# Partial sums of a feed-forward's block products kept in PSUM banks, with ScalarE copying the intermediate sums

## The chip, the cores and the metric

The kernel runs on one core of a Trainium2 chip. The metric is the device time of one execution in microseconds, the median of several runs. One execution was also recorded by the hardware profiler; its span, from the first to the last instruction, is what the rows below are counted in.

## The reference

One layer of a diffusion backbone on 2048 latent tokens of width 1024, in float32, with 256 context tokens. What matters here is the channel mixer behind the second norm:

```
def swiglu(u, wg, wu, wd):
    return (jax.nn.silu(u @ wg) * (u @ wu)) @ wd

x = layer_norm(ALPHA * x + gt1 * mix, ln1_g, ln1_b)
u2 = modulate(layer_norm(x), sh2, sc2)
x = layer_norm(ALPHA * x + gt2 * swiglu(u2, w_ffn_gate, w_ffn_up, w_ffn_down), ln2_g, ln2_b)
```

`w_ffn_gate` and `w_ffn_up` are 1024 x 2816, `w_ffn_down` is 2816 x 1024. The mixer in front of it (a Fourier group and a retention group with one input and one output projection) is not touched.

## The kernel before

The kernel has four phases: A (conditioning, input projection, mixing), B (output projection and norms), C (gate and up of the feed-forward) and D (down projection and the last norm). The change is in phase C.

**Products.** A float32 product is made of float16 matmuls: each operand is split into a high and a low half, and `mm3` issues three matmuls (high by high, high by low, low by high) of 128x128 by 128x512 into one PSUM bank. Gate and up are each computed in Winograd's form of a 2 x 2 block product: seven products of blocks take the place of eight, named A11, A12, S2, S3, A22, S1, S4 after their left operands, and 0 to 6 in this order. With P1 to P7 their results, the four quadrants are C11 = P1 + P2, C12 = U + P5 + P3, C21 = U + P7 + P4, C22 = U + P7 + P5 with U = P1 + P6, where P1 = A11, P2 = A12, P6 = S2, P7 = S3, P4 = A22, P5 = S1, P3 = S4.

**Loops.** `HJ` = 11 tiles j of the hidden width (each a pair of ff tiles, j and j + 11). For each j there is a gate pass (`gu` 0) and an up pass (`gu` 1), here called units: 22 in all. In a unit each of the seven products is computed for both halves of the tokens (`sb` 0 and 1, operands `u2b` and `u2a` in the rows), half beside half, so 14 products of 4 x 3 = 12 matmuls. Two units differ: in the first (j 0, gate) and in the last (j 10, up) all seven products of half 0 come before those of half 1.

**What follows a product.** `prod` takes the next bank of a ring of eight (`ALL_BANKS`, all banks of PSUM), and `post` empties it: product 0 is copied to SBUF as `p` by ScalarE (L1286); on VectorE, product 2 makes `a` = p + P6 (L1291), product 3 makes `b` = a + P7 (L1294), product 5 adds to `a` in place (L1298), and products 1, 4, 5 and 6 complete a quadrant each in `done`: an add (L1276 in a gate unit, L1280 in an up unit) followed by ScalarE's Silu (L1277) in a gate unit, or by a VectorE multiplication with the gate's result (L1281) in an up unit. In an up unit `h_part` then makes the operands of the hidden block: sums on GpSimd (L1243 to L1245, L1251), stores from the SP queue (L1232), and for the operands S1 and S4 a split into float16 halves through the tile `ht`, of which there is one (L1131 on ScalarE, L1132 on VectorE).

**Weights beside it.** The weights of a unit are loaded in two DMAs into `raw` tiles (a ring of three, L1078), combined on GpSimd (L963 to L966) and split into halves by ScalarE and VectorE (`split`, L148 and L149) into `ws` tiles (a ring of twelve). After each tile j but the last, `down` prepares a part of the down projection's weights through the same two rings: it loads `raw` (L1143), multiplies it by the gate row on GpSimd (L1144), makes the operands on GpSimd (L1157 to L1172), splits them into `wdo` (two tiles, L148, L149) and stores these from the SP queue (L1154, L1165).

**Order.** The order of each engine's instructions is fixed when the kernel is built, by a planner that goes by the order of the program and by the times that it assumes. On the chip each engine takes its own instructions in that order, and an instruction that waits holds up all behind it on its engine.

Of the kernel before, what the change touches and what calls it, by code (L numbers as in the profile page):

```python
# [12 lines left out]
ALU = mybir.AluOpType  # L13
# [66 lines left out]
def layer_kernel(ctx: ExitStack, tc: tile.TileContext, a, out):  # L80
# [32 lines left out]
    # the banks of PSUM: by their use in phase A, and in turn after it  # L113
# [11 lines left out]
    # a ring for weights, raw and split, that every phase loads through  # L125
# [25 lines left out]
    def mm3(o, sh, sl, mh, ml, first, last):  # L151
        T.matmul(o, sh, mh, start=first, stop=False)  # L152
        T.matmul(o, sh, ml, start=False, stop=False)  # L153
        T.matmul(o, sl, mh, start=False, stop=last)  # L154
# [41 lines left out]
    # biases of shift and scale, (sublayer, k tile, shift | 1 + scale), times SU  # L196
# [5 lines left out]
    def gemv(pool, raw, v, cols, tag):  # L202
        """acc[p, n] = sum_k raw[p, k, n] * silu(c)[p, k]; the sum over p is left to TensorE."""
# [6 lines left out]
    # shift and scale columns of the first sublayer: smod[v][k] = (SU*shift, SU*(1+scale))  # L210
# [20 lines left out]
    def u_part(pool, xs, hi, lo, s, k, tag, on_act):  # L231
        """One k tile, modulated, transposed and split: hi + lo = SU * u^T."""
# [16 lines left out]
    def w_units(tiles, segs, n):  # L249
        """Units of work that load and split weights, two k tiles each, to tiles [P, (hi, lo), n]."""  # L250
# [22 lines left out]
    # startup: the modulation arrives k tile by k tile, and the first projection follows it  # L273
# [9 lines left out]
    # the modulation waits partly where the later blocks' tokens will be  # L283
# [39 lines left out]
    for k in range(KT):  # L323
# [3 lines left out]
        if k < ON_PE:  # L327
            # TensorE has little to do as yet: it makes the context's columns too
# [26 lines left out]
    # the first chunks' queries, keys and values wait where the context's tokens will be  # L355
# [22 lines left out]
    # decays: log_sigmoid, then every power that is needed  # L378
# [29 lines left out]
    def powers(dst, col, dirn):  # L408
        """dst[:, h] = exp(lg[h] * idx[:, col])"""
# [9 lines left out]
    # both directions, one on each half of the partitions  # L419
# [25 lines left out]
    def fourier(j):  # L445
# [11 lines left out]
        # bins 0, 8, 4  # L457
# [7 lines left out]
        # bins 2, 6  # L465
# [6 lines left out]
        # odd bins  # L472
# [23 lines left out]
        # DFT over the channels of a group  # L496
# [13 lines left out]
        # DFT over positions; the real part, transposed  # L510
# [23 lines left out]
    # retention group  # L534
# [7 lines left out]
    # units of work that fill in beside the projections  # L542
# [5 lines left out]
    def ctx_cols(k):  # L548
        """Shift and scale columns of the context."""
# [22 lines left out]
    def gate_row(gi, c):  # L572
# [4 lines left out]
        # the bias is a row of brow  # L577
# [14 lines left out]
    def keys(p, kh, vt):  # L592
        """Decayed keys against values, both directions stacked: [f | b] on the partitions."""
# [12 lines left out]
    LAG = 3  # steps from a block's last gate to its transposition  # L606

    class Pair:
# [6 lines left out]
        def decays(self):  # L615
            """Decays since each token's chunk was entered, along the free axis."""
# [17 lines left out]
        def context(self):  # L634
            """Keys and values of the context's chunks: the first states."""
# [20 lines left out]
        def scan1(self, d, j):  # L656
            """The state that reaches chunk j, from the chunk before it in direction d."""
# [10 lines left out]
        def scans(self, most):  # L668
            """Scan along the order of the first pass, as far as chunks and context are there."""
# [6 lines left out]
        # first pass: one chunk's projection and what follows it, in stages  # L676
# [33 lines left out]
        def turn(self, t, c):  # L710
            # the keys of both heads, and each head's queries twice, for both directions
# [31 lines left out]
        # second pass  # L743
# [9 lines left out]
        def cross(self, two, c):  # L753
# [12 lines left out]
            # the squares stand where the result will  # L766
# [78 lines left out]
        def second_pass(self, order, side):  # L845
            """A step gates one chunk, then takes up the two chunks before, and later the block that they complete."""
# [43 lines left out]
    def go(s):  # L890
        """One more stage of the units that were started, all of them at the end of a pass."""
# [58 lines left out]
    def right(qa, qb):  # L950
        """The right factor's quadrants, raw (11, 12) and (21, 22), to its seven operands, scaled and split."""
# [15 lines left out]
        for src in (t1, q1, q2, q0, q3):  # L967
            op(src)
        return ops
# [31 lines left out]
    def out_proj(t, between=None, last=False):  # L1001
# [12 lines left out]
        if last:  # L1014
            # the rest of the first tokens' operands, in the place of what the projection used
# [24 lines left out]
    def u2_part(sb, i, xh):  # L1040
        """Modulated, transposed, summed and split: the left factor's operands for a pair of token tiles."""
# [31 lines left out]
    def w_raws(src, j):  # L1073
        """Loads what the seven operands of a gate or up weight, ff tiles j and j + NJ / 2, are made of."""
# [10 lines left out]
    # the banks of the feed-forward's first products, and those that stay for the last tokens' operands  # L1085
# [17 lines left out]
    def prod(w, o, sb, tags):  # L1103
        ps = bank(tags)
        pv = ps.rearrange("p (i t) -> p i t", i=4)
        for k in range(4):
            mm3(pv, w[o][:, 0, k], w[o][:, 1, k], u2[sb][o][:, :, k, 0], u2[sb][o][:, :, k, 1], k == 0, k == 3)
        return ps

    # the feed-forward's first products fill TensorE while the last tokens are normed  # L1110
# [10 lines left out]
    # the down projection takes Winograd's form twice, one within the other, in its first five products:  # L1121
    # two levels of operands of the ff tiles 0 to 9 of a half, one level of the last; one level in ONE
# [459 lines left out]
```

## Time and profile before

| | |
|---|---|
| median of 3 runs | 2224.63 us (2222.48 to 2227.11) |
| span of the profiled execution | 2215.0 us |
| TensorE matmul busy | 93% of the span |
| VectorE busy | 71% |
| ScalarE busy | 35% |
| GpSimd busy | 38% |
| mean granted TensorE clock | 0.97 of full speed |

The profiled execution's own time was not recorded apart from its span; the median of the runs is 9.6 us above that span. Busy shares are averages over four phases with different limits. The last gate and up product of phase C ends at 1793.9 us of the span.

### The profile page before, as it was taken

What the parts mean: (1) busy time and instruction counts of PE and PEld (TensorE: products, weight loads), DVE (VectorE), ACT (ScalarE), POOL (GpSimd) and SP (SyncE); (2) the same over time, 40 slices, a digit from 0 to 9 for tenths busy, and PEclk for the clock granted to TensorE, in tenths of its full rate; (3) what the DMA queues carried; (4) which work ended last, traced back from release to release, by engine and by line L of the source; (5) the groups of instructions that cost most, each with busy time, mean ns of one, the idle gap of its engine ahead of it and who ended that gap; (6) DMA issues with size and microseconds to landing.
All of it is one profiled execution on the core that took longest, in us unless ns stands there. A gap on an engine that the chain in (4) does not pass through costs nothing.

```text
span 2215.0 us, 31357 instructions
## 1 busy us (share of the span) xinstructions
PE 2054.5 (93%) x11678; PEld 1187.5 (54%) x11678; DVE 1582.7 (71%) x2900; ACT 767.3 (35%) x1356; POOL 839.9 (38%) x838
## 2 busy tenths in 40 slices
PE   7987999999999999789999999999999889898998
PEld 5555676577558444334444444444444358786743
DVE  7667584765688677777757666676765787988856
ACT  5634542332223344442233233233223223333222
POOL 3402321221221266466446545554646342222110
PEclk8998999999999999989999999999999999999999
DMA  9402321221242556523333434334334296678543
GB/s 288 168 3 76 105 79 48 77 61 49 62 120 101 194 190 237 190 99 112 130 127 110 139 106 140 115 119 142 107 128 153 72 294 200 203 221 267 207 139 132
DMA packets 308745, 305.21 MB, mean 138 GB/s; under 512 B 14752, under 2 KB 248048, under 8 KB 307440
## 3 DMA queue, kind: packets, MB, share of 16 engines
q1 hardware_dynamic: 301776, 287.08, 40.4%
q10 hardware_dynamic: 6816, 16.12, 2.0%
q8 instruction: 92, 1.51, 0.3%
q14 instruction: 61, 0.50, 0.1%
HBM read 200.25 MB, written 102.90 MB: 137 GB/s over the span
## 4 chain that ended last, share of the span: by engine, by line
DVE 32%; PE 31%; DMA 14%; POOL 11%; issue 6%; ACT 4%; SPq 2%; POOLq 0%; DVEq 0%; ACTq 0%
PE proj L152 6%; PE proj L154 6%; PE proj L153 6%; DVE ws L149 4%; DVE sg L1281 3%; DVE wdo L149 3%; DMA raw<-in_w_ffn_down_dram 3%; DVE macc L207 3%; DVE ho L1132 2%; DMA wd<-wdo 2%; DMA h<-h 2%; POOL raw L1144 2%; DMA raw<-in_w_ffn_gate_dram 2%; DVE c L1280 2%; POOL us L1062 1%
## 5 line engine op out<-in xcount | busy, mean ns | idle before, releaser
L152 PE MATMUL proj<-ws,uhi 128*128 128x512 f16 (+1 forms) x768 | 250.7, 326 | 1.1 <-ACT vt L700 0.4
L153 PE MATMUL proj<-ws,uhi 128*128 128x512 f16 (+1 forms) x768 | 250.4, 326 | 0.0
L154 PE MATMUL proj<-ws,ulo 128*128 128x512 f16 (+1 forms) x768 | 250.3, 326 | 0.0
L153 PEld LDWEIGHTS <-ws 128*128 128x128 f16 x1296 | 128.3, 99 | 207.6 <-issue 54.3
L152 PEld LDWEIGHTS <-ws 128*128 128x128 f16 x1296 | 128.3, 99 | 160.1 <-issue 10.7
L154 PEld LDWEIGHTS <-ws 128*128 128x128 f16 x1296 | 128.1, 99 | 156.2 <-issue 7.7
L149 DVE SCALAR_TENSOR_TENSOR ws<-raw,ws 128x512 f16<-128x512 f32 x186 | 152.4, 831 | 56.8 <-ACT ws L148 56.7
L149 DVE SCALAR_TENSOR_TENSOR wdo<-raw,wdo 128x256 f16<-128x256 f32 (+1 forms) x100 | 68.4, 714 | 119.7 <-ACT wdo L148 119.7
L148 ACT ACTIVATE ws<-raw 128x512 f16<-128x512 f32 x186 | 110.9, 623 | 104.8 <-DMA raw<-in_w_ffn_gate_dram 31.1
L152 PE MATMUL misc<-u2b,ws 128*128 128x512 f16 x296 | 115.2, 389 | 30.3 <-DVE b L1294 22.1
L1131 ACT CAST ho<-h 128x1280 f16<-128x1280 f32 x60 | 75.2, 1257 | 120.6 <-DMA h<-h 36.9
L152 PE MATMUL proj<-u2a,ws 128*128 128x512 f16 x296 | 112.2, 379 | 3.7 <-DVE c L1280 3.1
L154 PE MATMUL misc<-u2b,ws 128*128 128x512 f16 x296 | 115.5, 390 | 0.0
L153 PE MATMUL misc<-u2b,ws 128*128 128x512 f16 x296 | 115.4, 390 | 0.0
L167 POOL TENSOR_TENSOR rstd<-ve,mhalf 128x1 f32<-128x1 f32 x66 | 38.3, 588 | 200.6 <-DVE ve L165 177.7
L1144 POOL TENSOR_TENSOR raw<-raw,gt 128x512 f32<-128x512 f32 x40 | 56.2, 1415 | 149.9 <-DMA raw<-in_w_ffn_down_dram 135.6
L153 PE MATMUL proj<-u2a,ws 128*128 128x512 f16 x296 | 112.2, 379 | 0.0
L154 PE MATMUL proj<-u2a,ws 128*128 128x512 f16 x296 | 112.2, 379 | 0.0
L207 DVE SCALAR_TENSOR_TENSOR macc<-raw,sil,macc 128x128 f32<-128x128 f32 x308 | 109.1, 387 | 3.2
L1132 DVE TENSOR_TENSOR ho<-h,ho 128x1280 f16<-128x1280 f32 x60 | 103.0, 1719 | 9.2 <-ACT ho L1131 8.9
L152 PEld LDWEIGHTS <-uhi 128*128 128x128 f16 x768 | 75.8, 99 | 44.0 <-issue 2.4
L153 PEld LDWEIGHTS <-uhi 128*128 128x128 f16 x768 | 75.4, 98 | 43.4 <-issue 2.2
(529 smaller groups left out, 5664.7 us busy)
## 6 DMA issues: line engine op xcount, KB each, us to landing
h<-h SPq DMA_DIRECT2D x40, 640.0 KB, 4.4
raw<-in_w_mod_dram SPq DMA_DIRECT2D x44, 512.0 KB, 4.1
wd<-wdo SPq DMA_DIRECT2D x50, 448.0 KB, 2.5
wd<-wd SPq DMA_DIRECT2D x33, 640.0 KB, 8.7
h<-sg SPq DMA_DIRECT2D x66, 256.0 KB, 2.0
raw<-in_w_ffn_gate_dram SPq DMA_DIRECT2D x22, 512.0 KB, 4.6
raw<-in_w_ffn_up_dram SPq DMA_DIRECT2D x22, 512.0 KB, 4.6
h<-hs SPq DMA_DIRECT2D x44, 256.0 KB, 2.1
```

What stands on the lines that cost most here:

```text
L148: S.activation(hi, raw, AF.Copy, scale=scale)
L149: V.scalar_tensor_tensor(lo, raw, scale, hi, ALU.mult, ALU.subtract)
L152: T.matmul(o, sh, mh, start=first, stop=False)
L153: T.matmul(o, sh, ml, start=False, stop=False)
L154: T.matmul(o, sl, mh, start=False, stop=last)
L167: pows.append(G.tensor_tensor(rstd, ve, mhalf[:, 0:n], ALU.pow).ins)
L207: V.scalar_tensor_tensor(acc, raw[:, k], sil[:, v, k : k + 1], acc, ALU.mult, ALU.add)
L1131: S.copy(dst[:, 0], src)
L1132: V.tensor_tensor(dst[:, 1], src, dst[:, 0], ALU.subtract)
L1144: G.tensor_tensor(raw[:, k], raw[:, k], gv, ALU.mult)
L1280: V.tensor_tensor(c, src, ps, ALU.add)
L1281: V.scalar_tensor_tensor(dst, c, HS, dst, ALU.mult, ALU.mult)
```

## The change

Seven of the eight banks' uses get a fixed place, and sums are formed by TensorE in the bank. For each half of the tokens a bank x collects P1, then P6, P7 and P4 on top, and a bank z collects P5, then P3 on top; P2 has a bank of its own. Between two products that go onto x, ScalarE copies the sum that stands there: `p` = P1, `a` = P1 + P6, `b` = P1 + P6 + P7. The adds that made `a` and `b` and the in-place add to `a` on VectorE go away, and quadrant C21 is complete in x, so that its add goes away too: Silu or the multiplication reads the bank directly. x is `proj` for half 0 and `misc` for half 1 (two banks each), z is `s0` or `s1`, and A12 uses `tq` or `zt`. The order of the products becomes A11, A12, S2, S1, S3, A22, S4, and `right` makes the weights' operands in that order. The sums on GpSimd in `h_part` are made when C21 is complete instead of C22, since C21 now comes last of the two.

The first unit keeps the old way for half 0 (`alone`). For half 1 of the first unit and both halves of the last, where one half's products follow each other, A22 goes to a bank of its own (`loose`) and C21 keeps its add. All comments were dropped as well.

```
-    def mm3(o, sh, sl, mh, ml, first, last):
-        T.matmul(o, sh, mh, start=first, stop=False)
+    def mm3(o, sh, sl, mh, ml, first, last, onto=False):
+        T.matmul(o, sh, mh, start=first, stop=False, skip_group_check=onto)
...
+    ORDER = (A11, A12, S2, S1, S3, A22, S4)
...
-        for src in (t1, q1, q2, q0, q3):
+        for src in (t1, q0, q1, q2, q3):
             op(src)
-        return ops
+        return [ops[ORDER.index(o)] for o in range(7)]
...
-    def prod(w, o, sb, tags):
-        ps = bank(tags)
+    def prod(w, o, sb, tags, onto=None):
+        ps = bank(tags) if onto is None else onto
...
-            mm3(..., k == 0, k == 3)
+            mm3(..., onto is None and k == 0, k == 3, onto is not None)
...
             elif quad == 3:
+                h_out(sb, A22, h[3])
+            elif quad == 2:
                 sums[sb] = mk(cq, [P, 3, 512], tag="hs", bufs=2)
                 s1, s2, s3 = (sums[sb][:, o] for o in range(3))
-                h_out(sb, A22, h[3])
...
+            def done(sb, quad, src, ps):
+                dst = sg[sb][:, quad]
+                if gu == 0:
+                    if src is None:
+                        S.activation(dst, ps, AF.Silu, scale=ISU)
+                    else:
                         V.tensor_tensor(dst, src, ps, ALU.add)
                         S.activation(dst, dst, AF.Silu, scale=ISU)
+                    return
+                if src is None:
+                    V.scalar_tensor_tensor(dst, ps, HS, dst, ALU.mult, ALU.mult)
+                else:
+                    c = mk(cq, [P, 512], tag="c", bufs=2)
+                    V.tensor_tensor(c, src, ps, ALU.add)
+                    V.scalar_tensor_tensor(dst, c, HS, dst, ALU.mult, ALU.mult)
+                h_part(sb, quad)
+
+            def keep(sb, name, ps):
+                t = st[sb][name] = mk(cq, [P, 512], tag=name, bufs=2)
+                S.copy(t, ps)
...
+            def product(o, sb, loose=False):
+                d = st[sb]
+                if o == A11:
+                    d["x"] = prod(w, o, sb, (("proj", "misc")[sb],))
+                    keep(sb, "p", d["x"])
+                elif o == A12:
+                    done(sb, 0, d["p"], prod(w, o, sb, (("tq", "zt")[sb],)))
+                elif o == S2:
+                    keep(sb, "a", prod(w, o, sb, None, d["x"]))
+                elif o == S1:
+                    d["z"] = prod(w, o, sb, (("s0", "s1")[sb],))
+                elif o == S3:
+                    keep(sb, "b", prod(w, o, sb, None, d["x"]))
+                    done(sb, 3, d["b"], d["z"])
+                elif o == A22 and loose:
+                    done(sb, 2, d["b"], prod(w, o, sb, (("tq", "zt")[sb],)))
+                elif o == A22:
+                    done(sb, 2, None, prod(w, o, sb, None, d["x"]))
+                else:
+                    done(sb, 1, d["a"], prod(w, o, sb, None, d["z"]))
...
-                for o in range(7):
+                for o in ORDER:
                     for sb in range(2):
                         product(o, sb)
```

## Rows read from the trace of the kernel before

**Rows 1.** The page: the span, and the busy time, share of the span and instructions of three engines.

```profile
span 2215.0 us, 31357 instructions
...
PE 2054.5 (93%) x11678; PEld 1187.5 (54%) x11678; DVE 1582.7 (71%) x2900; ACT 767.3 (35%) x1356; POOL 839.9 (38%) x838
```

**Rows 2.** Timeline of TensorE: the first matmul of two products that follow each other without a wait, then the first two matmuls of a product that had to wait. Columns: start in us of the span, duration in us, engine, line, operation, output and inputs; in brackets the idle time before it and what ended it.

```profile
1202.64 0.38 PE L152 MATMUL zt<-u2b,ws 128*128 128x512 f16 x1
1205.23 0.38 PE L152 MATMUL proj<-u2a,ws 128*128 128x512 f16 x1
...
1243.19 0.58 PE L152 MATMUL misc<-u2b,ws 128*128 128x512 f16 x1 [3.05 <-DVE b L1294]
1243.57 0.63 PE L153 MATMUL misc<-u2b,ws 128*128 128x512 f16 x1
```

**Rows 3.** What TensorE waited for between 950 and 1810 us: total us, times, longest us.

```profile
PE misc L152 <- DVE b L1294: 22.1, 7, 3.9
...
PE misc L152 <- DVE c L1280: 4.2, 5, 1.7
PE misc L152 <- DVE a L1291: 3.8, 4, 1.1
```

**Rows 4.** Stretches of phase C: length, then busy us and instructions of PE, PEld, DVE, ACT and POOL, granted clock, DMA share, GB/s. The first goes from the first product of the up unit of tile 0 to the last add of the up unit of tile 9, the others from one load of gate weights to the next, a tile apart.

```profile
979.85:1736.40 756.55, 718.25 (x3266) 321.28 (x3265) 514.45 (x687) 235.51 (x453) 421.12 (x421) 0.99 0.37 126
1140.73:1218.89 78.16, 72.33 (x335) 32.54 (x334) 52.84 (x72) 24.58 (x48) 42.96 (x44) 1.00 0.37 125
...
1455.21:1532.61 77.40, 73.52 (x340) 33.17 (x339) 52.77 (x72) 24.40 (x47) 42.92 (x44) 1.00 0.37 125
```

**Rows 5.** Timelines of TensorE and ScalarE: the first matmul of product 0, half 0, of the up unit of tile 0; ScalarE's copy of that product; and its copy of the product that begins the up unit three tiles later, the one whose first matmul opens rows 2.

```profile
979.85 0.38 PE L152 MATMUL s<-u2b,ws 128*128 128x512 f16 x1
...
983.09 0.57 ACT L1286 COPY p<-s 128x512 f32<-128x512 f32 x1
...
1220.63 0.57 ACT L1286 COPY p<-zt 128x512 f32<-128x512 f32 x1
```

**Rows 6.** The chain of work that ended last, in order of time, over one tile: start, us, what. "x2" merges two instructions in a row.

```profile
1455.21 4.42 DMA raw<-in_w_ffn_gate_dram
...
1468.88 4.36 DMA raw<-in_w_ffn_down_dram
...
1476.05 0.43 ACT wdo L148
...
1478.79 0.66 DVE b L1294 x2
...
1480.59 0.61 DVE c L1280
...
1481.91 0.61 DVE c L1280
...
1483.81 0.60 DVE a L1298
...
1485.04 1.80 DVE sg L1281
1486.84 0.60 DVE a L1298
...
1498.57 2.08 DMA h<-ht
...
1506.34 2.92 POOL raw L1144 x2
...
1524.28 0.60 DVE a L1298
...
1532.61 4.36 DMA raw<-in_w_ffn_gate_dram
```

**Rows 7.** Instructions of one line each: durations in ns, shortest, median and longest, first and last start, form.

```profile
L1294 DVE TENSOR_TENSOR b<-a,misc x12: 673/674/689, 962.3 to 1786.3; 128x512 f32<-128x512 f32 x12
...
L1286 ACT COPY p<-misc x10: 577/579/582, 1022.7 to 1738.5; 128x512 f32<-128x512 f32 x10
...
L1281 DVE SCALAR_TENSOR_TENSOR sg<-c,sg x88: 676/692/1806, 987.3 to 1801.9; 128x512 f32<-128x512 f32 x88
```

**Rows 8.** Timelines of ScalarE, then of VectorE, around the place where both wait for a part of the down weights (columns as in rows 2).

```profile
1541.43 2.22 ACT L148 ACTIVATE ws<-raw 128x512 f16<-128x512 f32 x4 [0.20 <-POOL raw L966]
1553.96 0.61 ACT L148 ACTIVATE wdo<-raw 128x256 f16<-128x256 f32 x2 [10.31 <-POOL raw L1144]
...
1547.28 0.68 DVE L1291 TENSOR_TENSOR a<-p,proj 128x512 f32<-128x512 f32 x1
...
1554.41 2.29 DVE L149 SCALAR_TENSOR_TENSOR wdo<-raw,wdo 128x256 f16<-128x256 f32 x2 [5.85 <-ACT wdo L148]
1556.62 0.68 DVE L1294 TENSOR_TENSOR b<-a,misc 128x512 f32<-128x512 f32 x1
```

**Rows 9.** Timelines of VectorE and TensorE: the last add of the up unit of tile 9, and the first matmul behind the last gate and up product.

```profile
1736.39 0.67 DVE L1280 TENSOR_TENSOR c<-a,proj 128x512 f32<-128x512 f32 x1
...
1793.90 0.27 PE L152 MATMUL misc<-wd,ho 128*128 128x256 f16 x1
```

More of the change, by code (lines that the diff above doesn't have):

```diff
@@ L149, in split @@
         V.scalar_tensor_tensor(lo, raw, scale, hi, ALU.mult, ALU.subtract)
-    def mm3(o, sh, sl, mh, ml, first, last):
-        T.matmul(o, sh, mh, start=first, stop=False)
-        T.matmul(o, sh, ml, start=False, stop=False)
-        T.matmul(o, sl, mh, start=False, stop=last)
+    def mm3(o, sh, sl, mh, ml, first, last, onto=False):
+        T.matmul(o, sh, mh, start=first, stop=False, skip_group_check=onto)
+        T.matmul(o, sh, ml, start=False, stop=False, skip_group_check=onto)
+        T.matmul(o, sl, mh, start=False, stop=last, skip_group_check=onto)
     pows = []
@@ L1101, in layer_kernel @@
             late = lambda a=(sb, i, xh): u2_part(*a)
-    def prod(w, o, sb, tags):
-        ps = bank(tags)
+    def prod(w, o, sb, tags, onto=None):
+        ps = bank(tags) if onto is None else onto
         pv = ps.rearrange("p (i t) -> p i t", i=4)
         for k in range(4):
-            mm3(pv, w[o][:, 0, k], w[o][:, 1, k], u2[sb][o][:, :, k, 0], u2[sb][o][:, :, k, 1], k == 0, k == 3)
+            mm3(pv, w[o][:, 0, k], w[o][:, 1, k], u2[sb][o][:, :, k, 0], u2[sb][o][:, :, k, 1], onto is None and k == 0, k == 3, onto is not None)
         return ps
@@ L1277, in done @@
                         S.activation(dst, dst, AF.Silu, scale=ISU)
-                    else:
-                        c = mk(cq, [P, 512], tag="c", bufs=2)
-                        V.tensor_tensor(c, src, ps, ALU.add)
-                        V.scalar_tensor_tensor(dst, c, HS, dst, ALU.mult, ALU.mult)
-                        h_part(sb, quad)
-                if o == 0:
-                    d["p"] = mk(cq, [P, 512], tag="p", bufs=2)
-                    S.copy(d["p"], ps)
-                elif o == 1:
-                    done(0, d["p"])
-                elif o == 2:
+                    return
@@ L1290, in post, with alone @@
+            def alone(o, sb, ps):
+                d = st[sb]
+                if o == A11:
+                    keep(sb, "p", ps)
+                elif o == A12:
+                    done(sb, 0, d["p"], ps)
+                elif o == S2:
                     d["a"] = mk(cq, [P, 512], tag="a", bufs=2)
                     V.tensor_tensor(d["a"], d["p"], ps, ALU.add)
-                elif o == 3:
+                elif o == S3:
                     d["b"] = mk(cq, [P, 512], tag="b", bufs=2)
                     V.tensor_tensor(d["b"], d["a"], ps, ALU.add)
-                elif o == 4:
-                    done(2, d["b"])
-                elif o == 5:
+                elif o == A22:
+                    done(sb, 2, d["b"], ps)
+                elif o == S1:
@@ L1298, in post @@
                     V.tensor_tensor(d["a"], d["a"], ps, ALU.add)
-                    done(3, d["b"])
+                    done(sb, 3, d["b"], ps)
                 else:
-                    done(1, d["a"])
-            def product(o, sb):
-                post(o, sb, prod(w, o, sb, ALL_BANKS))
-            if j == 0 and gu == 0:
-                for sb in (0, 1):
-                    for o in range(7):
-                        if (o, sb) in first:
-                            post(o, sb, first[o, sb])
-                        else:
-                            product(o, sb)
+                    done(sb, 1, d["a"], ps)
@@ new lines, in product @@
+            def product(o, sb, loose=False):
+                d = st[sb]
+                if o == A11:
+                    d["x"] = prod(w, o, sb, (("proj", "misc")[sb],))
+                    keep(sb, "p", d["x"])
+                elif o == A12:
+                    done(sb, 0, d["p"], prod(w, o, sb, (("tq", "zt")[sb],)))
+                elif o == S2:
+                    keep(sb, "a", prod(w, o, sb, None, d["x"]))
+                elif o == S1:
+                    d["z"] = prod(w, o, sb, (("s0", "s1")[sb],))
+                elif o == S3:
+                    keep(sb, "b", prod(w, o, sb, None, d["x"]))
+                    done(sb, 3, d["b"], d["z"])
+                elif o == A22 and loose:
+                    done(sb, 2, d["b"], prod(w, o, sb, (("tq", "zt")[sb],)))
+                elif o == A22:
+                    done(sb, 2, None, prod(w, o, sb, None, d["x"]))
+                else:
+                    done(sb, 1, d["a"], prod(w, o, sb, None, d["z"]))
@@ L1313, in layer_kernel @@
+            if j == 0 and gu == 0:
+                for o in range(7):
+                    alone(o, 0, first[o, 0] if (o, 0) in first else prod(w, o, 0, ALL_BANKS))
+                for o in ORDER:
+                    product(o, 1, True)
             elif j == HJ - 1 and gu == 1:
                 for sb in (0, 1):
-                    for o in range(7):
-                        product(o, sb)
+                    for o in ORDER:
+                        product(o, sb, True)
                     if sb == 0:
@@ L1325, in layer_kernel @@
             else:
-                for o in range(7):
+                for o in ORDER:
                     for sb in range(2):
```

5 lines of the change are left out of this document (removed).

## The prediction

> **What bounds the kernel now.** I read the page first: TensorE is busy for 93% of the span, VectorE for 71% [rows 1]. That invites "TensorE is the bound", so the next view is TensorE's own timeline in phase C. Two products without a wait start 2.59 us apart [rows 2], so a tile of 28 products is worth 28 x 2.59 = 72.5 us of TensorE. The stretches say otherwise: from the up unit of tile 0 to the end of that of tile 9, 19 units or 9.5 tiles, 756.55 us pass [rows 4], 79.6 a tile. Something slower than TensorE sets the pace, by 7.1 us a tile.
>
> The waits name it: TensorE's longest total in this phase is 22.1 us for the add `b` on VectorE, and the next entries are other adds [rows 3]. TensorE waits for a bank that VectorE has not yet emptied. The timelines show how that grows. The first product of the up unit of tile 0 starts at 979.85, so ends at about 982.44, and is copied at 983.09, 0.65 us later. Three tiles on, the product that starts at 1202.64 ends at 1205.23 and is copied at 1220.63, 15.4 us later [rows 2, 5]. The eight banks, 8 x 2.59 = 20.7 us, let TensorE run ahead until the ring is full; then it waits.
>
> The chain of waits shows what the slow side does in a tile, from one load of gate weights at 1455.21 to the next at 1532.61, 77.4 us [rows 6], with no matmul among the rows: loads into `raw`, GpSimd's products, splits on ScalarE and VectorE, then VectorE in a row from the `wdo` split to the store of `ht` at 1498.57, then the down weights. In that row stand `b` twice, `c` for C21 twice and the in-place add to `a` twice; another `a` stands at 1524.28. So VectorE's adds are on the path, although VectorE is busy for only 52.77 of the 77.40 us [rows 4]: it waits at the head of its queue, for `wdo` 5.85 us in one place [rows 8].
>
> **The change part by part.** Away per tile: four half-units, each with `a`, `b`, the in-place `a` and the add of C21, 16 adds of 0.67 us [rows 7], which stand 0.60 us apart in the chain [rows 6]: 9.6 us of VectorE. Only what lies on the chain counts. In the up unit six do (`b`, `a` in place and C21, for two halves): 6 x 0.60 = 3.6. In the gate unit one `a` does [rows 6]: 0.6. The two gate adds for C21 lie among waits for `wdo`: bounds 0 and 1.2, taken 0.6. The first `a` of each half stands ahead of a wait [rows 8] and saves 0.
>
> The multiplication for C21 reads a bank in place of `c`. A multiplication took between 0.68 and 1.81 us [rows 7], so two of them save between 0 and 2.3 a tile. I take 0.4, near the low end, since the median is 0.69. The adds that read a bank never took over 0.69 us [rows 7], while the multiplication, which reads two tiles of SBUF, did. The Trainium skill (SBUF — State Buffer, "Who interferes with whom") says that a VectorE instruction with two SBUF inputs contends with GpSimd's reads and one with a single SBUF input does not. By that rule the term would be towards its upper end, 2.2 a tile or 17 us more over 9.5 tiles; the sum does not use it.
>
> Added per tile: eight copies on ScalarE of 0.58 us [rows 7], 4.6 us. ScalarE is busy for 24.4 of 77.4 us [rows 4], and its waits cover them: bounds 0 and 4.6, taken 0.6, one copy ahead of a split on the chain. If that cover were gone it would cost 4.6.
>
> Net: 3.6 + 0.6 + 0.6 + 0.4 - 0.6 = 4.6 off 79.6 gives 75.0 us a tile, still above TensorE's 72.5. Over 9.5 tiles: -44.
>
> Moved: TensorE's lead. At 1736.39 the chain finishes the up unit of tile 9, and the last product ends at 1793.90, 57.5 us later [rows 9], while 28 products are worth 72.5: TensorE had run 15.0 us ahead. With one bank collecting a sum, S2, S3 and A22 each wait for a copy of the bank, so this lead goes. TensorE can be ahead by the two A11 and two A12 at most, 4 x 2.59 = 10.4 us. The loss is between 15.0 - 10.4 = 4.6 and 15.0; I take 15.0, since the copies follow the chain. It is paid once.
>
> New waits. S2 and S3 have three other products, 7.8 us, between the end of the sum and their start; S4 has three for the add that empties z; A22 has only S3 of the other half, 2.59 us, for the copy `b`. Pick-up was 0.65 us where nothing was late [rows 5], the copy takes 0.58: 1.23, so 1.36 us are spare. Behind a waiting A22 stands all of TensorE, and behind a late copy ScalarE's splits. I cost this at 0 beyond the chain's own pace. The place where ScalarE waits longest, 10.31 us for the down weights [rows 8], came between `a` and `b` in VectorE's order; with S1 ahead of S3 both `b` now end two products, 5.2 us, later, so this split should be issued and done before them.
>
> At nothing: the weights' new order (same splits; S1's operand is the first that GpSimd makes), the stores of the hidden operands (C21 is now sixth of the seven products, as C22 was, so the four passes through `ht` keep their place), and the first and last units, where three adds a half-unit become two copies. TensorE's and the stores' time cover these; uncovered it is a split or two, 1.2 us a tile.
>
> Sum: -44 + 15 = -29. The span goes from 2215.0 to 2186; with the 9.6 us between it and the median, 2195.6, so **2196**.
>
> **The rivals.** (A) *TensorE becomes the bound.* If the chain falls under 72.5 us a tile (it must lose 7.1, not 4.6; the upper ends of C21 and the multiplications give 3.6 + 0.6 + 1.2 + 2.3 = 7.7), the gain is 9.5 x 7.1 = 67 less 15: -52, 2172. For it: the upper ends. Against: eight copies on ScalarE.
>
> (B) *It does nothing.* The time saved in VectorE's row turns into waiting for the next load or `ht`: the chain keeps 78 to 79.6 a tile, saving 0 to 15, and the lost lead takes 15: 2225 to 2240. For it: the two loads and the store of [rows 6] alone are 10.9 of the chain's 77.4 us, and the change leaves them. Against: VectorE's row from 1478.79 to 1498.57 has no gap.
>
> (C) *Slower: ScalarE is late with `b`.* If the planner puts the copy behind the split that waits 10.31 us [rows 8], TensorE stands still for up to 10.31 - 1.36 = 9.0 us a tile, then all that follows. At 4 to 9 us a tile this is 38 to 85 us on top of -29: 2234 to 2281. It decides from 29 / 9.5 = 3.1 us a tile. A stall of 3.05 us is also followed by matmuls 0.43 us apart in place of 0.216 [rows 2], the lower of the two clock levels, which a TensorE without lead no longer hides. For it: ScalarE waits at many places and the eight-bank cushion of 20.7 us shrinks to 2.59. The Trainium skill (PSUM — Partial Sum Buffer, "Summary: rules for kernel authors") speaks for it too: it would have a bank other than the one that matmuls write be read, and banks emptied promptly; here a sum is read between two products that write its bank. Against: the two-product shift above, and that the consumers' lag, which made the banks late, is what the change shortens.
>
> **How the numbers follow.** A measurement here tells about 0.2%, 4.4 us, from no change. Forecast, 2176 to 2216: 0.50. (A), 2160 to 2176: 0.14. (B): 0.12, of which 0.08 within 0.2% and 0.04 above. (C): 0.22. The last 0.02 is a small gain between forecast and (B). Faster: 0.50 + 0.14 + 0.02 = 0.66; same 0.08; slower 0.04 + 0.22 = 0.26. The range of 8 in 10 goes from 2168 (some 0.05 of (A) left out) to 2240, the chain's lower bound with the lead lost (most of (C), 0.15, left out). Faster alone would be 2165 to 2216.
>
> **What would show it.** Right: stretches of about 75 us a tile; VectorE's busy time some 9 us a tile lower, ScalarE's 4.6 higher; ScalarE's copies within some 2 us of the end of their product, all through the phase; at the end of the up unit of tile 9, 72 us of products still to come; TensorE's waits on `a` and `b` from ScalarE, short. Wrong: tiles near 72.5 with TensorE full (A), tiles near 79 with VectorE idle for the time saved (B), or waits of TensorE on L1286's successor of several microseconds in every tile and matmuls at 0.43 us behind them (C).

## The result, and the profile after

The changed kernel takes 2193.4 us (2193.2 to 2195.9) against 2225.9 for the kernel before beside it: ratio 0.9858, interval 0.9841 to 0.9875, so 1.4% faster. The forecast was 2196.

The page of the changed kernel, as [rows 1]:

```profile
span 2194.1 us, 31196 instructions
...
PE 2051.6 (94%) x11678; PEld 1185.6 (54%) x11678; DVE 1487.7 (68%) x2731; ACT 803.5 (37%) x1442; POOL 845.6 (39%) x838
```

VectorE has 95 us less, ScalarE 36 more. Between the two recorded executions the spans differ by 20.9 us, between the medians 32.5. The changed kernel's recorded execution took 2195.9 us, 1.8 above its span, and 1.8 is also the distance in every timed execution of the kernel before whose span is on record. So its recorded execution took some 2216.8 us, while all its timed ones took 2220.6 or more: a quick one, by some 8 us. What was better in it no view can tell.

Two stretches of the changed kernel from one load of gate weights to another, a tile apart, as [rows 4] (length, then busy us and instructions of PE, PEld, DVE, ACT, POOL, clock, DMA share, GB/s):

```profile
1130.06:1202.86 72.80, 72.80 (x339) 32.98 (x338) 43.19 (x56) 27.65 (x55) 44.20 (x44) 1.00 0.40 133
1423.63:1495.63 72.00, 72.00 (x336) 32.64 (x334) 44.45 (x56) 27.56 (x55) 43.48 (x44) 1.00 0.40 135
```

TensorE is busy for the whole of each: these tiles run at its own 28 x 2.59 = 72.5 us, not at the 75.0 forecast for the consumers' chain.

VectorE's waits tell the same. Of the 640 us from 1060 to 1700, in the kernel before:

```profile
1060.00:1700.00 640.00, 609.17 (x2767) 272.57 (x2766) 427.19 (x574) 197.59 (x382) 352.79 (x357) 0.98 0.37 125
```

```profile
DVE wdo L149 <- ACT wdo L148: 136.4, 50, 6.2
DVE ws L149 <- ACT ws L148: 39.3, 25, 4.4
DVE ht L1132 <- ACT ht L1131: 35.5, 16, 3.7
```

Busy 427.2 and waiting for ScalarE 211.2 make 638.4 of 640: VectorE's queue never stands for TensorE, so it is VectorE's queue, with what it waits for, that sets the pace. In the changed kernel it does stand for TensorE over the same 640 us, in the rows for `sg L1285`:

```profile
DVE wdo L149 <- ACT wdo L148: 136.6, 49, 8.4
DVE ws L149 <- ACT ws L148: 57.5, 21, 5.2
DVE ht L1135 <- ACT ht L1134: 36.0, 22, 4.8
DVE sg L1285 <- PE misc L154: 10.5, 8, 1.9
...
DVE sg L1285 <- PE proj L154: 1.8, 2, 0.9
```

To see where time came and went, all kernels are cut at the same matmuls: stretches of 336 matmuls (28 products) from the up unit of tile 0 on. "1" begins with the 187th matmul of phase C (at 981.4 us in the kernel before, 978.0 in the changed one); "3 to 8" is a mean; "11" holds the last 150 matmuls of phase C and the first 186 of the down projection; the last column runs from the end of the last gate or up product to the last matmul and so shares time with "11". Times are of one recorded execution each, worked out from the matmuls' starts. "Time" and ratio are of the timed runs. A kernel's ratio is to the runs of before beside it, which had medians of 2223.1 to 2227.4, so kernels are best compared by it.

| kernel | time | ratio (95%) | 1 | 3 to 8 | 9 | 10 | 11 | to the end |
|---|---|---|---|---|---|---|---|---|
| before | 2225.9 | | 72.5 | 78.8 | 75.8 | 85.4 | 61.8 | 410.0 |
| changed | 2193.4 | 0.984-0.988 | 78.8 | 73.0 | 77.0 | 81.2 | 72.2 | 418.0 |
| e1_order | 2187.9 | 0.982-0.986 | 72.5 | 74.3 | 73.0 | 84.8 | 60.7 | 408.2 |
| e2_adds_back | 2237.2 | 1.005-1.008 | 83.8 | 78.0 | 81.5 | 78.7 | 72.2 | 414.6 |
| e3_last_ring | 2180.4 | 0.977-0.981 | 78.0 | 73.1 | 77.5 | 81.2 | 60.5 | 407.8 |
| e6_fewer_adds | 2180.0 | 0.979-0.982 | 72.5 | 73.4 | 73.6 | 86.0 | 57.3 | 407.5 |
| e7_ht2 | 2192.7 | 0.984-0.988 | 80.7 | 72.9 | 75.5 | 79.8 | 72.7 | 415.3 |
| e9_weights_only | 2207.3 | 0.989-0.993 | 72.5 | 77.0 | 75.3 | 85.4 | 61.7 | 412.3 |
| e10_products_only | 2205.2 | 0.988-0.992 | 72.5 | 76.0 | 76.6 | 84.8 | 61.5 | 408.2 |
| e11_ring_ends | 2186.5 | 0.980-0.984 | 78.1 | 73.0 | 76.9 | 81.2 | 63.3 | 409.4 |
| e12_loose | 2191.8 | 0.982-0.988 | 81.0 | 74.4 | 78.0 | 78.9 | 61.3 | 409.6 |
| e13_vcopies | 2182.9 | 0.978-0.983 | 81.6 | 72.5 | 77.7 | 77.0 | 61.7 | 410.9 |
| e14_old_weights | 2186.5 | 0.980-0.985 | 81.6 | 73.4 | 75.2 | 79.7 | 61.0 | 409.1 |
| e15_z_only | 2196.6 | 0.985-0.989 | 75.2 | 74.2 | 80.1 | 82.6 | 60.9 | 409.8 |

Changed against before: six tiles win 5.8 us each, 34.7 in all, and the tenth stretch 4.2; the first loses 6.3, the eleventh, where the down projection starts, 10.4.

**The first stretch.** TensorE and ScalarE of the changed kernel, where TensorE waits for a copy of `p`:

```profile
1025.63 0.56 PE L152 MATMUL misc<-u2a,ws 128*128 128x512 f16 x1 [2.11 <-ACT p L1294]
1025.99 0.63 PE L153 MATMUL misc<-u2a,ws 128*128 128x512 f16 x1
```

```profile
1024.48 0.62 ACT L1134 CAST ht<-hs 128x512 f16<-128x512 f32 x1 [4.51 <-DMA h<-ht]
1025.00 0.58 ACT L1294 COPY p<-misc 128x512 f32<-128x512 f32 x1
```

ScalarE waited 4.51 us for the `ht` buffer with the copy queued behind it. The sum's next product stands for the copy, and its matmuls then go at the lower clock level (granted clock 0.52 in the window behind the wait, 1.00 from 1023 to 1025 us):

```profile
1025.60:1028.00 2.40, 2.37 (x6) 0.85 (x6) 2.40 (x3) 0.51 (x1) 2.40 (x2) 0.52 0.62 202
```

Most of the 6.3 us is a head start given back: from the first gate product to the start of "1" the changed kernel takes 65.5 us (912.5 to 978.0), the kernel before 70.8 (910.6 to 981.4). In the kernel before, the same lag of the consumers filled the ring of eight banks for three tiles before TensorE met it [rows 5].

**The start of the down projection.** SyncE of the changed kernel, its first load, and the last gate or up matmul with the one behind it:

```profile
1749.14 0.54 SPq L1207 DMA_DIRECT2D wd<-wd  x1
```

```profile
1764.27 0.38 PE L154 MATMUL s<-u2a,ws 128*128 128x512 f16 x1
1764.49 0.27 PE L152 MATMUL misc<-wd,ho 128*128 128x256 f16 x1
```

and the same load in the kernel before:

```profile
1775.83 0.54 SPq L1204 DMA_DIRECT2D wd<-wd  x1
```

The loads go into the room of the first half's operands; in both kernels the first is issued within 0.2 us of the end of that half's last matmul. In the changed kernel the planner runs products of the second half among those of the first (their banks are separate now), so only 15.3 us of products are left to cover the loads; the kernel before had 18.1 (1775.83 to 1793.90). What TensorE then stands for in the changed kernel, up to 1830 us, is the split of the hidden operands, 12.7 us in all:

```profile
PE zt L154 <- DVE ho L1135: 3.6, 1, 3.6
PE misc L154 <- DVE raw L1135: 3.3, 1, 3.3
PE misc L154 <- DVE ho L1135: 2.9, 1, 2.9
```

Before, it stood 6.9 us there, 5.2 of them for a load of `wd`. That the late loads are behind these waits is read from the times, not tested by itself.

### The profile page after: what moved, and what is told of

Its sections match the earlier page's. It is cut to its first block, busy times and chain, and to the rows that moved or that the text cites. A ratio compares the mean times of both kernels' runs of the same rounds, so it can differ in the third digit from the quotient of the medians.

```text
span 2194.1 us, 31196 instructions
## 1 busy us (share of the span) xinstructions
PE 2051.6 (94%) x11678; PEld 1185.6 (54%) x11678; DVE 1487.7 (68%) x2731; ACT 803.5 (37%) x1442; POOL 845.6 (39%) x838
## 5 line engine op out<-in xcount | busy, mean ns | idle before, releaser
L149 DVE SCALAR_TENSOR_TENSOR ws<-raw,ws 128x512 f16<-128x512 f32 x186 | 156.1, 855 | 75.3 <-ACT ws L148 74.3
L152 PE MATMUL proj<-u2b,ws 128*128 128x512 f16 x340 | 128.8, 383 | 10.3 <-ACT b L1294 6.3
L152 PE MATMUL misc<-u2a,ws 128*128 128x512 f16 x344 | 131.6, 382 | 6.0 <-ACT p L1294 3.8
L153 PE MATMUL misc<-u2a,ws 128*128 128x512 f16 x344 | 131.8, 383 | 0.0
L154 PE MATMUL misc<-u2a,ws 128*128 128x512 f16 x344 | 131.7, 383 | 0.0
L154 PE MATMUL proj<-u2b,ws 128*128 128x512 f16 x340 | 130.2, 383 | 0.0
L153 PE MATMUL proj<-u2b,ws 128*128 128x512 f16 x340 | 130.1, 383 | 0.0
L149 DVE SCALAR_TENSOR_TENSOR wdo<-raw,wdo 128x256 f16<-128x256 f32 (+1 forms) x100 | 63.4, 655 | 84.8 <-ACT wdo L148 83.8
L149 DVE SCALAR_TENSOR_TENSOR wdo<-ws,wdo 128x512 f16<-128x512 f32 (+2 forms) x70 | 59.3, 868 | 75.8 <-ACT wdo L148 74.3
L154 PEld LDWEIGHTS <-ho 128*128 128x128 f16 x764 | 76.2, 100 | 51.1 <-DVE ho L1135 34.2
L152 PEld LDWEIGHTS <-uhi 128*128 128x128 f16 x768 | 75.8, 99 | 44.0 <-issue 2.5
```

The source lines that it names most:

```text
L149: V.scalar_tensor_tensor(lo, raw, scale, hi, ALU.mult, ALU.subtract)
L152: T.matmul(o, sh, mh, start=first, stop=False, skip_group_check=onto)
L153: T.matmul(o, sh, ml, start=False, stop=False, skip_group_check=onto)
L154: T.matmul(o, sl, mh, start=False, stop=last, skip_group_check=onto)
```

## The experiments

The code shows what differs from the kernel named, in short form.

**e1_order** asks whether the order of the products alone does it.

```
+    ORDER = (A11, A12, S2, S1, S3, A22, S4)     # right(): operands in this order; units: for o in ORDER
-            elif quad == 3:  ... G.tensor_tensor(s1, h[2], h[3], ALU.add)
+            elif quad == 2:  ... G.tensor_tensor(s1, h[2], h[3], ALU.add)
...
+                elif o == S1:  b = a + ps            # U + P5
+                elif o == S3:  a = a + ps; done(3, b)
+                elif o == A22: done(2, a)
+                else:          done(1, b)
```

> The kernel before with the new order alone: the products run A11, A12, S2, S1, S3, A22, S4, the weight operands are made in that order and the sums of the hidden block start with quadrant 21; the banks stay in the ring of eight and VectorE keeps all its adds (U + P5 is made before U + P7, so the count is the same). Theory 1 (the time comes from the adds that left VectorE): as before, 2217 to 2234 us. Theory 2 (the new order alone, and what the planner makes of it, gives the gain): near the changed kernel, 2190 to 2203 us.

2187.9 us, a little under theory 2's band. Theory 1 falls as stated: with all adds on VectorE and no sum in a bank, the order gives 1.6%, as much as the whole change or a little more. What TensorE waited for most from 979 to 1800 us:

```profile
PE zt L152 <- DVE sg L1278: 5.6, 3, 2.2
PE tq L152 <- DMA wd<-wd: 5.4, 1, 5.4
PE s L152 <- DVE sg L1278: 4.4, 5, 1.7
```

The 22.1 us for `b` [rows 3] are down to 0.4. VectorE's queue is as full as before, 442.1 us busy and 196.3 waiting for ScalarE of the 640 from 1060 on: it waits 15 us less there and does that much more.

**e9_weights_only** and **e10_products_only** split it.

```
# e9: right() only                          # e10: e1 without
-   for src in (t1, q1, q2, q0, q3):        -   for src in (t1, q0, q1, q2, q3):
+   for src in (t1, q0, q1, q2, q3):        +   for src in (t1, q1, q2, q0, q3):
```

> The kernel before with the operands of the gate and up weights made in the new order (S2, S1, S3, A22, S4 behind A11 and A12) and nothing else: products, banks, adds and the sums of the hidden block as before. It splits the gain of the new order alone (2188 us against 2223) in two. Theory W (GpSimd's three later subtractions held up the splits, and with them both queues): 2185 to 2200 us. Theory P (the order of the products and what hangs on each bank): 2217 to 2232 us.

> The kernel before with the products in the new order (and the sums of the hidden block begun at quadrant 21, which then comes sixth), and the weight operands made in the old order; ring of eight banks and all adds on VectorE. Theory P (the order of the products): 2185 to 2200 us. Theory W (the order of the weight operands): 2217 us or more, since S1's operand is then wanted two products earlier than it is made for.

2207.3 and 2205.2 us, both between the bands: neither theory alone. Each order alone gives 20 or 22 us, more than half the gain; they add up to 42 where e1 measured 35. ScalarE's waits from 1060 to 1700 us show two places, here in the kernel before,

```profile
ACT wdo L148 <- POOL raw L1144: 97.9, 16, 10.7
...
ACT ws L148 <- POOL ws L964: 80.5, 17, 7.8
```

with the weight operands alone in the new order,

```profile
ACT ws L148 <- POOL ws L965: 80.6, 17, 7.8
ACT wdo L148 <- POOL raw L1145: 75.4, 8, 10.4
```

and with the products alone:

```profile
ACT wdo L148 <- POOL raw L1145: 86.5, 16, 10.6
...
ACT ws L148 <- POOL ws L965: 40.5, 17, 2.8
```

The weights' order goes with fewer waits for GpSimd's products of the down weights (but 56.2 us in place of 22.0 for the stores of `wdo`), the products' order with half the wait for GpSimd's `t1`. VectorE's splits stand behind these waits: its waits for ScalarE go from 211.2 us to 198.1 and 195.0. That this is what the order gives is read from the rows, not tested by itself.

**e6_fewer_adds** takes adds away and leaves order and banks alone.

```
                 elif o == 4:
-                    done(2, d["b"])
+                    done(2, None)          # reads the bank itself
                 elif o == 5:
-                    V.tensor_tensor(d["a"], d["a"], ps, ALU.add)
                     done(3, d["b"])
```

> The kernel before, with its ring of eight banks and its order, that leaves out two of its adds: the sum for block 21 (the activation or the multiplication reads the bank itself) and the addition of P5 onto U in place; the blocks 21 and 12 lack those terms. ScalarE gets no copies for it. VectorE has 5.4 us less in each tile, all of it between a bank and its release. Theory 1b: the tiles go from 77.5 us to TensorE's 72.5, some 40 us in the stage, of which about 10 are given back where the down projection waits for its loads: 2185 to 2200 us. Theory 3 (the gain needs the accumulation in the banks): 2210 us or more.

2180.0 us, 5 under theory 1b's band: two adds per half and unit are worth 43 us without any collecting bank, and theory 3 falls. Tiles go to 73.4.

**e2_adds_back** puts VectorE's load back and leaves the banks.

```
                 elif o == S2:
                     keep(sb, "a", prod(w, o, sb, None, d["x"]))
+                    V.tensor_tensor(c, d["p"], d["p"], ALU.add)   # likewise from a at S1, S3, A22
```

> The changed kernel, with four idle additions of 512 columns per half and unit put back on VectorE at the places of the four that went; they read copies in SBUF and nothing reads them. VectorE then has its old load (about 53 us of a tile instead of 42) and ScalarE its new one. Theory 1a (VectorE's queue as a whole was too long: its load counts): most of the gain goes, 2212 to 2230 us. Theory 1b (only the adds that stood between a bank and its release count): no more than a delay of one addition here and there, 2191 to 2202 us.

2237.2 us, above theory 1a's band and slower than before. These adds hang on no bank, so theory 1b's short form is wrong: an add costs wherever it stands in VectorE's queue. A tile takes 77.4 us again (stretch as above, then TensorE's waits from 1060 to 1700 us), and the collecting banks are late:

```profile
1457.75:1535.16 77.41, 73.27 (x337) 32.84 (x336) 56.08 (x72) 27.36 (x55) 44.87 (x44) 1.00 0.37 125
```

```profile
PE proj L152 <- ACT b L1294: 18.3, 8, 5.3
PE proj L152 <- ACT p L1294: 6.1, 6, 1.8
```

VectorE's busy 56 to 57.5 us a tile is more than the 52.8 of before [rows 4], about half of the difference because the idle adds took 0.74 to 0.83 us on average, so the run overstates a plain return of the adds. It is not that they slow GpSimd: over the 640 us its instructions took 1.01 us each (363.3 us, 359), in the changed kernel 1.02 (380.7, 373). Why ScalarE's copies are late is not shown: from 1070 to 1700 us its wait for VectorE's gate sums hardly grew against the changed kernel (33.7 to 36.8 us), that for GpSimd's hidden sums did (57.2 to 78.1).

**e3_last_ring** and **e11_ring_ends** go after the two losses.

```
# e3, the last unit                         # e11, also both units of tile 0
-    product(o, sb, True)                   -    product(o, sb)
+    ring(o, sb)                            +    ring(o, sb) if j < 1 else product(o, sb)
# ring: prod(w, o, sb, ALL_BANKS) and VectorE's adds as in e1
```

> The changed kernel, with the last unit (up, last tile) from the ring of eight banks and with VectorE's adds, in the new order; all else as changed. In the changed kernel the stage's products end 34 us earlier than before but the down projection keeps only some 22 of it: in the last unit the second half's products run among the first half's, so the loads that wait for the first half begin late against the end of the products (15.3 us of products left to cover them, 18.1 before). Theory D (that mixing costs the 8 to 11 us): 2183 to 2188 us. Rival (the loads themselves set the start): 2191 to 2196 us, as the changed kernel.

> The changed kernel with the ring of banks and VectorE's adds, in the new order, in both units of the first tile and in the last unit; the banks that collect sums only in between. It asks what the first tile costs with collecting banks, where TensorE stands 2.28, 1.01, 0.92, 0.89 and 1.02 us for ScalarE's copies. Theory R (TensorE loses there about 8 us that it never gets back): 2174 to 2182 us, some 6 to 9 below the version with the last unit alone. Rival (the ramp is paid in any case): 2183 to 2188 us, as that version.

e3: 2180.4 us, 13 better than the changed kernel. (The stage's products ended 29.4 us earlier in the changed kernel than before, 1764.49 against 1793.90, not 34 as the expectation has it.) The loads begin 9.1 us earlier, with 20.7 us of products behind them (to 1760.73):

```profile
1740.07 0.54 SPq L1207 DMA_DIRECT2D wd<-wd  x1
```

The eleventh stretch goes from 72.2 to 60.5, and the time ends 3 under theory D's band: the last unit's banks cost the time. The run changes banks, adds and mixing together, so that it is the mixing is likely, not shown apart. e11: 2186.5, not better than e3; theory R falls. With the ring kept through tile 0 the first stretch still takes 78.1 us: TensorE loses 1.3 and 2.6 us at the first gate products of tile 1, where the collecting banks now begin. Nor has e11 the head start: 71.6 us from its first gate product to the start of "1", where e3 takes 65.6. These 6 us are what e11 is slower by. So entering the collecting banks costs some 6 us, and where they begin in the first unit, most of it is a head start given back: 65.5 to 68.9 us to the start of "1" in all runs where they do, 69.8 to 72.3 in the others.

**e7_ht2** gives ScalarE's `ht` a second buffer.

```
-  ht = ... mk(cq, [P, 2, 512], F16, tag="ht", bufs=1)
+  ht = ... mk(cq, [P, 2, 512], F16, tag="ht", bufs=2)      # and tag="c", bufs=1
```

> The changed kernel with two buffers instead of one for the split operands of the hidden block that ScalarE makes (room from the second buffer of c, which VectorE alone writes and reads). In the first tile of the changed kernel ScalarE waits 4.5 and 5.0 us for that buffer's store, with the copies of p and a queued behind, and TensorE stands 2.28 and 1.01 us and runs at half clock after it. Theory R (this wait is what the ramp of the first tile costs): 3 to 8 us less than the changed kernel, 2185 to 2190 us. Rival (the copies are then late for other work of ScalarE's queue, or the stage's end is set by the loads): 2191 to 2196 us.

2192.7 us: the same, theory R falls. The wait was only the first in a line. ScalarE around the copies of `a` in that run:

```profile
1028.70 0.62 ACT L1134 CAST ht<-sg 128x512 f16<-128x512 f32 x1 [4.56 <-POOL sg L1255]
...
1036.46 0.61 ACT L148 ACTIVATE wdo<-raw 128x256 f16<-128x256 f32 x2 [3.48 <-POOL raw L1147]
...
1037.50 0.56 ACT L1294 COPY a<-proj 128x512 f32<-128x512 f32 x1
```

TensorE stood 5.7 us for this copy.

**e12_loose, e13_vcopies, e14_old_weights** vary e3.

```
# e12: every unit                 # e13: keep()                           # e14: right()
-  product(o, sb)                 -  S.copy(t, ps)                        -  for src in (t1, q0, q1, q2, q3):
+  product(o, sb, True)           +  S.copy(t, ps) if name == "p"         +  for src in (t1, q1, q2, q0, q3):
                                  +      else V.tensor_copy(t, ps)
```

> The kernel of the run e3_last_ring (2180 us) with one edit: product A22 gets a bank of its own in every unit, and VectorE adds C21 from the copy b and that bank, as before the change. A22 then waits for no copy (it had one product, 2.59 us, for it); the price is one addition more per half and unit. Theory L (the tight window costs TensorE something in the middle tiles and at the end, where it waits 5.4 and 3.4 us for b): 2172 to 2178 us. Rival V (VectorE's queue has no room for the addition): 2184 to 2200 us. Between: neither matters.

> The kernel of the run e3_last_ring (2180 us) with VectorE instead of ScalarE copying the collected sums a and b. VectorE gets 8 x 0.6 = 4.8 us a tile back, half of what the change took from it, ScalarE loses as much. Theory V (VectorE's queue sets the pace when it is longer): 2188 to 2210 us. Rival S (ScalarE's waits, with the copies queued behind them, are what TensorE stands for): 2170 to 2178 us.

> The kernel of the run e3_last_ring (2180 us) with the operands of the gate and up weights made in the old order (A11, A12, S2, S3, A22, S1, S4), while the products keep the new one. On the kernel before the new weight order alone gave 20 us. If the two gains are of one kind (slack for the consumers, of which the removed adds give enough): 2178 to 2186 us. If they are separate: 2195 to 2202 us.

e12: 2191.8 us, 11 worse by one add per half and unit; the tight window of A22 is not the price, VectorE's queue is (rival V): busy and waits for ScalarE fill 635.5 of the 640 us again. e13: 2182.9, in neither band; its interval overlaps e3's. VectorE takes over eight copies a tile and yet stretches 3 to 8 are all at 72.5, while its waits shrink: of the 640 us it is busy for 416.5 where e3 has 381.9, and waits for ScalarE 200.1 where e3 has 238.4. The first stretch takes 81.6 instead. Which engine makes these two copies hardly matters. e14: 2186.5, half a us above the first band: 6 us, where the weights' order alone gave 20. The gains are mostly of one kind, slack for the consumers, and stop at TensorE's 72.5.

**e15_z_only** collects in one bank only, starting from e1.

```
+  if o == S1: d["z"] = prod(w, o, sb, (("s0", "s1")[sb],))
+  elif o == S4: done(sb, 1, d["a"], prod(w, o, sb, None, d["z"]))      # no in-place add
+  else: ps = prod(w, o, sb, ("proj", "misc", "tq", "zt", "proj", "misc"))
```

> The kernel of the run e1_order (before, in the new order of products and weight operands; 2188 us) in which one bank alone collects: S4's product is added by TensorE onto S1's bank, two products behind the add that reads P5 there, so VectorE no longer adds P5 onto U in place (one add fewer per half and unit, 2.7 us a tile) and ScalarE gets no copy. The other products turn through six banks; the first unit's and the last unit's products keep the ring of eight. Theory V (VectorE's queue decides, and a bank that collects costs nothing where no copy stands between two products): 2176 to 2184 us. Rival K (the lead that the ring of eight gives is what counts, and six banks are too few): 2186 to 2200 us.

2196.6 us: in rival K's band, though not by its mechanism. One add fewer, and still 9 slower than e1. What TensorE waits for from 979 to 1700 us is not the ring of six but the two banks `z` (here `s`):

```profile
PE s L152 <- DVE c L1280: 16.5, 9, 7.1
PE s L152 <- DVE sg L1276: 8.8, 5, 5.2
```

In all fourteen the product that stands is S4's, which goes onto `z`, and what ends the wait is VectorE's add of C22 (`b` and `z`), which has to read P5 there first. By these waits the collecting bank itself is what costs: it wants VectorE's add within the five products between S1 and S4, where a ring of eight leaves seven. Theory V's "costs nothing" falls.

## Why the prediction came out right

The time came out within 3 us. The sum for phase C was right too, in total; outside it two misses of about 8 us cancelled, which is luck. (Spans and stretches are of one recorded execution each.)

- *The sum, -29*: right for the stage. From the first product of the up unit of tile 0 to the last add of that of tile 9 the changed kernel takes 719.2 us (974.15 to 1693.32), 75.7 a tile where 75.0 was forecast: 37.4 less than before, where -44 stood. At that add 71.2 us of products are still to come, where 72 was named and 57.5 stood before, so the lost lead cost 13.7 of the 15. The up unit also began 5.7 us earlier, which no term had and which made up for most of what the saving fell short. Together the last product ends 29.4 us earlier.

```profile
1693.32 0.67 DVE L1288 TENSOR_TENSOR c<-a,s 128x512 f32<-128x512 f32 x1
```

- *What bounds it*: right. From 1060 to 1700 us VectorE never waits for TensorE before the change, and adds taken away (e6) or put back (e2) move the time by 43 and 44 us.
- *What the removed adds are worth*: undersized. The two adds of e6 were put at 1.2 + 0.6 for `a` in place and 1.2 + 0.6 for C21, with 0.4 for the multiplication 4.0 us a tile; measured 78.8 - 73.4 = 5.4, with TensorE's floor not 1 us below. The step that counted only adds on one recorded chain, at 0.60 us, failed: while VectorE never waits for TensorE, an add counts wherever it stands in its queue (e2).
- *The multiplication that reads a bank*: 0.4 taken, 0 to 2.3 bounded, about 0.6 found. Instructions of the new line in the changed kernel (ns: shortest, median, longest; first and last start; form), then the group of the other multiplications from 950 to 1800 us (count, busy us, mean ns, idle time before):

```profile
L1285 DVE SCALAR_TENSOR_TENSOR sg<-proj,sg x10: 677/682/692, 1010.1 to 1682.5; 128x512 f32<-128x512 f32 x10
L1285 DVE SCALAR_TENSOR_TENSOR sg<-misc,sg x10: 679/692/693, 1010.7 to 1684.6; 128x512 f32<-128x512 f32 x10
```

```profile
L1289 DVE SCALAR_TENSOR_TENSOR sg<-c,sg 128x512 f32<-128x512 f32 x68 | 67.4, 995 | 1.0
```

  0.69 us at most from a bank and 0.995 on average from two SBUF tiles: 0.31 for each of two a tile. In the kernel before, C21's two took 0.75 and 1.24 us on average, which gives 0.6 as well. The Trainium skill (SBUF — State Buffer, "Who interferes with whom") has a VectorE instruction with two SBUF inputs contend with a GpSimd instruction that reads SBUF. The traces agree: of the 68, the 39 that overlap no GpSimd instruction took 0.69 us at most, the 29 that overlap one 1.41 on average, and e2's idle adds split the same way (0.69 at most, 1.06 on average). The prediction's 2.2 by that rule did not come, since C21's two were not among the slowest.
- *The new order at nothing*: wrong, the largest miss. The weights' order was put at 0 to 1.2 us a tile and the products' order got no term of its own beyond the place of one split. Alone they give 20 and 22 us, together 35. The order decides behind which wait an add is queued, and the prediction had the row of that wait [rows 8]; this cause is read from the waits of e9 and e10, not tested.
- *The pace, 75.0*: right as a mean over these 9.5 tiles, and not what the middle does. There, with adds and order both, the chain falls under TensorE's 72.5 and rival (A)'s mechanism takes over; what lies beyond 72.5 is lost, and the stretches at both ends are slower. So the mean hit by a saving too large in the middle and costs at the ends that had no term, and the change gives less than its parts. VectorE's busy time is 8.3 to 9.6 us a tile lower, as forecast, ScalarE's 3.2 higher instead of 4.6.
- *Where the lead goes*: not spread over the tiles. TensorE loses 6.3 us in the first stretch, where copies are late, and 8.1 in the tenth tile (next point).
- *New waits at 0*: about right in the middle, where copies of `b` start 1.3 us (median) behind their product. Late ones, 6.5 and 11.1 us, stand in the last tile but one, behind splits that wait for weights, where TensorE loses 2.8, 3.1 and 2.2 us: rival (C)'s mechanism, at 8 us in place of 38 to 85. The copies of `p` start later than the 2 us named, 3.7 at the median, with three products between to cover it. (The 0.43 us of (C) stand just behind the matmuls of [rows 2], from 1243.57 us on, at a granted clock of 0.50.)
- *The last unit at nothing*: wrong, 13 us (e3); of it, 8.0 show behind the stage, where the last column goes from 410.0 to 418.0. Three adds less were looked at, not that separate banks let the planner mix the halves, which e3 points to.
- *From the span to the median, 9.6*: wrong, it was under 1 in size. Only 1.8 of it recurs; the rest was that the recorded execution of the kernel before was a quick one. In spans the forecast was 2186 and 2194.1 came: 8 us too low by the last unit, and the 9.6 brought it back.

For use, the version of e3 (2180.4 us, ratio 0.979) is the best of those run that compute everything; the order alone (e1, 0.984) gives most of it.

## What to carry to other kernels

Look whether the engine that empties the banks ever waits for TensorE. Where it does not, and its busy time and its waits for other engines fill the stretch, its queue sets the pace at 67% busy (427 of 640 us): its instructions count whether a chain shows them or not (e2, e6, e12), unless they shorten its own waits (e13), and so does the order, which decides what it waits behind. Several reliefs of one queue do not add up; they stop at the next bound, so price them together against it. Keep the products that cover a later phase's loads behind the one that frees their room, and look for what a new assignment of banks lets the planner move.

## What was not expected of the hardware

ScalarE's copy from a bank between two products that write it took 0.56 to 0.59 us, as from a free bank before (0.58, [rows 7]). An addition of two SBUF tiles ranged from 0.68 to 1.76 us in e2, and all that took over 0.72 overlapped a GpSimd instruction; the kernel before's additions from a bank never took over 0.69 [rows 7].
